# A seven-product matrix step in a decoder layer: one sum of weight blocks by an accumulating DMA, more such steps, and one more block in the ring

## The chip, the cores and the metric

The kernel runs on one core of one Trainium2 chip. Its time is the device time in microseconds of one execution. Before the change three runs gave 1696.13, 1696.37 and 1696.46 us; the median, 1696.37 us, is the number to compare with. The chip profiler recorded one further execution.

The engines are called PE (matrix products; PEld is its weight loading), DVE (element-wise work on tensors), ACT (activation functions and copies), POOL (here a few small operations and the DMAs that its queue issues) and SP (which only issues DMAs). SBUF is the on-chip memory, PSUM the memory that PE writes its sums to.

## The reference

The layer works on 256 tokens of width 2048, all in float32:

```python
h = h + 0.5 * swiglu(rmsnorm(h, ffn1_norm), ffn1_w_in, ffn1_w_out)
u = rmsnorm(h, mix_norm) @ w_in_mix            # pool part, q, k, v, gate, low-rank decay
h = h + concat(pool_mixer(u), gla_mixer(u)) @ w_out_mix
h = h + 0.5 * swiglu(rmsnorm(h, ffn2_norm), ffn2_w_in, ffn2_w_out)
out = rmsnorm(h, final_norm)

def swiglu(h, w_in, w_out):                    # w_in 2048 x 11264, w_out 5632 x 2048
    gate, up = split(h @ w_in)
    return (silu(gate) * up) @ w_out
```

Nearly all work is in the two feed-forward parts: each has 23 million weights in `w_in` and 11.5 million in `w_out`, applied to only 256 rows. The mixer between them has five smaller projections, a pooling branch and a linear attention over chunks of 64 tokens.

## The kernel before

**Precision.** PE multiplies float32 numbers with one rounded factor at a time, so every operand x is kept as two tiles: `hi`, x rounded to PE's format, and `lo`, the rest x - hi. A product of blocks is three matmuls, hi*hi + hi*lo + lo*hi (the function `three`, L193). The activations' pairs stay in SBUF. Weights are read once: a step's weights arrive in a raw slot (`ring_raw`, loaded by SP at L137), ACT casts them to `ring_hi` (L157), DVE subtracts for `ring_lo` (L158).

**Steps.** The tokens are two tiles of 128 rows, the output columns of a group two tiles of 512, and the inner dimension is taken 256 at a time. A step is therefore a 2 x 2 block matrix of activations times a 2 x 2 block matrix of weights (4 blocks of 128 x 512, 1 MB). There are two ways to do it:

- an S step (`Group.s`) does the eight block products, 24 matmuls, and needs the four weight blocks as they are: 4 ring blocks;
- a W step (`Group.w`) does seven products by Winograd's variant of Strassen's scheme, 21 matmuls, with sums of blocks on both sides. The sums of activations (S1 to S4, tiles `s_f`, `s_z`) are made once for each 256-deep slice and used in every chunk. The sums of weight blocks (T1 to T4) are made by DVE for every step, in place in the raw slot, at L181 (`less` in `w_step`). It takes 7 ring blocks: B11, B22, B21 and T1 to T4. Four products go to separate PSUM banks (`pw_...`), and at the end of a group DVE combines them (`combine`, L307 to L310) and adds them to the accumulators (L495).

**Stages.** Each feed-forward part (function `ffn`; names with `f` for the first, `z` for the second) goes through 11 chunks of 512 hidden columns. `first_product(c)` multiplies by `w_in`, eight steps whose kinds stand in `KINDS`, then SiLU, the product with the up half, transposes on PE (`ftp`, `ztp`) and a split into hi and lo. After each chunk but the first and the last, `second_product` multiplies two finished chunks by one half of `w_out` in four S steps (two after chunk 1), halves the result on ACT (`half_f`, `half_z`) and adds it to `hd` in DRAM by an accumulating DMA that POOL issues (L549). The period of the middle of either part is thus one chunk and four S steps. The last two second products keep their result on the chip. `finish2` applies the last norm.

**Buffers.** In the feed-forward parts there are 4 raw slots (3 in the mixer and in the very last group) and a ring of 22 blocks (16 in the mixer and in the last groups), used in turn (class `Ring`); a step whose blocks straddle the ring's end is split into smaller instructions. The order of instructions on each engine is fixed when the program is built, by a scheduler that follows a model of their times; at run time every engine goes through its own list, in order, with semaphore waits. SP's list holds the loads, POOL's the `hd` additions.

The lines that the change touches most:

## Time and profile before

| | |
|---|---|
| median of three runs | 1696.37 us |
| the profiled execution, its own time | 1695.52 us |
| its span, first to last instruction | 1693.7 us |
| PE busy | 1680.2 us |
| DVE busy | 1485.8 us |
| ACT busy | 1022.3 us |
| POOL busy | 69.2 us |
| mean busy share of the 16 DMA engines in the middle of the second feed-forward part | 0.70 to 0.71 |
| granted PE clock, mean over the span | 0.998 of full speed |

A row of the groups reads: line, engine, operation, output<-inputs, shapes, count, then busy time, mean duration in ns, idle time before and what ended it. A matmul's duration (390 ns) overlaps that of the next; what counts is the distance of two starts. A row of the waits reads: who waited, for whom, us in total, times, the longest. A row of the windows reads: the window and its length, then for PE, PEld, DVE, ACT and POOL the busy time and the number of instructions, then the granted clock, the DMA engines' share and GB/s. A row of the DMA issues gives the count, the size of one and the median time from issue to landing.

### The profile page before, as it was taken

The page shows a single profiled execution, that of the slowest core. Times are in us where ns is not written, and L with a number is a line of the kernel's source. Part 1 is how long each engine was busy: PE and PEld are TensorE (multiplying, and loading weights), DVE is VectorE, ACT ScalarE, POOL GpSimd, SP SyncE. Part 2 cuts the span into 40 slices and gives each one's busy share as a digit, 9 for nine tenths or more (in the row PEclk, how much of TensorE's full clock was granted, in tenths as well). Part 3 has the DMA queues.
Part 4 walks back from the last instruction along what each step waited for, and adds up shares of the span by engine and source line. Part 5 has one row for each costly group of instructions (what it writes and reads, how often), then busy time and mean ns, then how long its engine had stood idle before and what let it go on. Part 6 is the DMA issues. An engine that isn't in the chain of part 4 may idle for free.

```text
span 1693.7 us, 21023 instructions
## 1 busy us (share of the span) xinstructions
PE 1680.2 (99%) x7669; PEld 1396.0 (82%) x7669; DVE 1485.8 (88%) x1663; ACT 1022.3 (60%) x1310; POOL 69.2 (4%) x74
## 2 busy tenths in 40 slices
PE   9999999999999999999999999999999999999997
PEld 7888888888888888888898888888888888888886
DVE  8779999999999996767968888999999999999974
ACT  7656666665665664565566565566566566566643
POOL 0000000000000000000000000000000000000012
PEclk9999999999999999999999999999999999999999
DMA  9856756856867776654576484767767667577681
GB/s 344 346 142 226 244 167 236 260 166 235 258 170 223 262 208 235 230 177 140 193 236 230 148 293 152 217 227 218 212 221 227 204 235 235 176 241 242 204 292 51
DMA packets 106330, 369.50 MB, mean 218 GB/s; under 512 B 11873, under 2 KB 15073, under 8 KB 106226
## 3 DMA queue, kind: packets, MB, share of 16 engines
q1 hardware_dynamic: 97026, 335.63, 57.8%
q0 software_dynamic: 8480, 31.46, 8.8%
q8 instruction: 60, 0.98, 0.2%
q10 hardware_dynamic: 720, 1.07, 0.2%
q14 instruction: 44, 0.36, 0.1%
HBM read 340.85 MB, written 27.26 MB: 217 GB/s over the span
## 4 chain that ended last, share of the span: by engine, by line
PE 97%; DMA 1%; DVE 0%; issue 0%; ACT 0%; SPq 0%; POOL 0%; POOLq 0%; DVEq 0%; ACTq 0%
PE ps_fi L193 18%; PE ps_zi L193 16%; PE ps_fo L193 14%; PE ps_zo L193 14%; PE pw_zi L193 9%; PE pw_fi L193 9%; PE ps_h L193 4%; PE pw L193 2%; PE ps_mg L193 2%; PE ps_mv L193 2%; PE ps_mp L193 2%; PE ps_mq L193 1%; PE ps_w_mk L193 1%; PE ps_w_mgr L193 1%; DMA ring_raw<-in_ffn_w_in 1%; PE ztp L511 1%
## 5 line engine op out<-in xcount | busy, mean ns | idle before, releaser
L157 ACT CAST ring_hi<-ring_raw 128x1024 fp32r<-128x1024 f32 (+3 forms) x952 | 837.7, 921 | 524.5 <-DMA ring_raw<-in_ffn_w_in 75.5
L158 DVE TENSOR_TENSOR ring_lo<-ring_raw,ring_hi 128x1024 fp32r<-128x1024 f32 (+5 forms) x794 | 964.3, 1242 | 154.4 <-ACT ring_hi L157 153.7
L181 DVE TENSOR_TENSOR ring_raw<-ring_raw 128x512 f32<-128x512 f32 (+1 forms) x366 | 313.3, 869 | 0.9
L193 PE MATMUL ps_fi<-ring_lo,xT_hi 128*128 128x512 f32 x386 | 150.5, 390 | 0.0
L193 PE MATMUL ps_fi<-ring_hi,xT_hi 128*128 128x512 f32 x386 | 147.8, 391 | 1.6 <-ACT ring_hi L157 1.6
L193 PE MATMUL ps_fi<-ring_hi,xT_lo 128*128 128x512 f32 x386 | 149.4, 389 | 0.0
L193 PE MATMUL ps_zi<-ring_lo,h_hi 128*128 128x512 f32 x362 | 141.0, 389 | 0.0
L193 PE MATMUL ps_zi<-ring_hi,h_lo 128*128 128x512 f32 x362 | 140.9, 390 | 0.0
L193 PE MATMUL ps_zi<-ring_hi,h_hi 128*128 128x512 f32 x362 | 139.7, 390 | 0.5 <-DVE h_mid L1040 0.5
L193 PE MATMUL ps_fo<-ring_lo,fhi 128*128 128x512 f32 x352 | 138.1, 392 | 0.0
L193 PE MATMUL ps_fo<-ring_hi,flo 128*128 128x512 f32 x352 | 137.3, 391 | 0.0
L193 PE MATMUL ps_fo<-ring_hi,fhi 128*128 128x512 f32 x352 | 137.0, 391 | 0.0
L193 PE MATMUL ps_zo<-ring_hi,zhi 128*128 128x512 f32 x344 | 134.9, 392 | 0.0
L193 PE MATMUL ps_zo<-ring_hi,zlo 128*128 128x512 f32 x344 | 134.8, 392 | 0.0
L193 PE MATMUL ps_zo<-ring_lo,zhi 128*128 128x512 f32 x344 | 134.3, 390 | 0.5 <-DVE ring_lo L158 0.5
L193 PE MATMUL pw_zi<-ring_hi,s_z 128*128 128x512 f32 x342 | 116.2, 389 | 0.0
L193 PE MATMUL pw_fi<-ring_hi,s_f 128*128 128x512 f32 x318 | 108.5, 389 | 0.0
L193 PEld LDWEIGHTS ps_fi<-ring_hi,xT_hi 128*128 128x128 f32 x386 | 72.5, 188 | 17.3 <-ACT ring_hi L157 2.3
L193 PEld LDWEIGHTS ps_fi<-ring_lo,xT_hi 128*128 128x128 f32 x386 | 72.6, 188 | 15.6 <-DVE ring_lo L158 0.7
L193 PEld LDWEIGHTS ps_fi<-ring_hi,xT_lo 128*128 128x128 f32 x386 | 72.6, 188 | 15.0
L193 PEld LDWEIGHTS ps_zi<-ring_hi,h_hi 128*128 128x128 f32 x362 | 68.0, 188 | 14.9 <-ACT ring_hi L157 0.9
L193 PEld LDWEIGHTS ps_zi<-ring_hi,h_lo 128*128 128x128 f32 x362 | 67.9, 188 | 14.0
(331 smaller groups left out, 2572.2 us busy)
## 6 DMA issues: line engine op xcount, KB each, us to landing
ring_raw<-in_ffn_w_in SPq DMA_DIRECT2D x350, 512.0 KB, 5.3
ring_raw<-in_ffn_w_out SPq DMA_DIRECT2D x176, 512.0 KB, 5.6
ring_raw<-in_w_out_mix SPq DMA_DIRECT2D x32, 512.0 KB, 5.0
hd<-half_f POOLq DMA_DIRECT2D x18, 512.0 KB, 8.1
hd<-half_z POOLq DMA_DIRECT2D x18, 512.0 KB, 8.3
ring_raw<-in_w_mv SPq DMA_DIRECT2D x16, 512.0 KB, 4.3
ring_raw<-in_w_mp SPq DMA_DIRECT2D x16, 512.0 KB, 4.7
ring_raw<-in_w_mg SPq DMA_DIRECT2D x16, 352.0 KB, 3.6
```

The costliest lines, as they stand in the source:

```text
L157: nc.scalar.copy(out=hi[:, j:k, :], in_=src[:, i + j : i + k, :])
L158: nc.vector.tensor_tensor(out=lo, in0=src[:, i : i + n, :], in1=hi.bitcast(F32), op=ALU.subtract)
L181: nc.vector.tensor_tensor(out=out, in0=x, in1=y, op=ALU.subtract)
L193: nc.tensor.matmul(ps, x, y, start=start and i == 0, stop=stop and i == 2, **kw)
L511: nc.tensor.transpose(tp[:, t, k, :], a_t[t][:, k * P : (k + 1) * P], ident)
```

## The change

1. **The weight sums of a W step.** The blocks of a step lie in memory in another order (B12, B11, B22, B21 instead of B11, B12, B22, B21; the array is built on the host). When the first half is loaded, POOL issues a DMA that reads B11 once more from DRAM (256 KB) and adds it onto B12 in the raw slot. The four sums are rewritten around that block (called Q1; signs in `combine` turn accordingly), so that DVE does two subtractions, one of 512 and one of 1024 columns, instead of three.
2. **More W steps.** Chunks 3 to 10 of both parts have seven W steps and one S step instead of six and two. Chunk 1 of the first part has three W steps instead of none. The last group of all (`zo`, chunks 9 and 10 by the second half of `w_out`) does its two steps of chunk 9 as W steps. This needs a seventh set of activation sums, made in chunk 2 and written over parts of the activations that are not read any more, and sums of chunk 9's hidden columns.
3. **The ring** has 23 blocks in the feed-forward parts instead of 22; one block is skipped at two places (`SKIP`).
4. **Order in the mixer.** The decay factors are computed inside the projection for v, which now precedes that for q; the attention scores move into the projection for the pooling branch.
5. **Small buffers**: `tmp` has three buffers under one tag instead of two under each of two tags.
6. **The end**: the last scalings of the output are held behind the last addition to h (`issue_after`).

```diff
-W_PAIRS = (1, 3, 4, 6, 2, 5)
-CHUNKS = ("WWWWWWSS",) * 8
+W_PAIRS = (1, 3, 4, 6, 2, 5, 0)
+CHUNKS = ("WWWWWWWS",) * 8
 KINDS = {
-    "f": ("SSSSSSSS", "SSSSSSSS", "WWSWWWSS") + CHUNKS,
+    "f": ("SSSSSSSS", "SSSWSWWS", "WWSWWWSS") + CHUNKS,
     "z": ("SSSSSSSS", "SWSWWWSS", "WWSWWWSS") + CHUNKS,
 }
...
-MORE_RING = 6
+MORE_RING = 7
...
+SKIP = {("f", 1): 1, ("f", 2): 1}
+SEVENTH_AT = 2
+SUMS_AT = 2
+LAST = {"f": (2, 3, 0, 1), "z": (0, 1, 2, 3)}
+LAST_W = (9,)
...
-        return lambda k, n: b[n if k == 0 else 3 - n]
+        return lambda k, n: b[1 - n if k == 0 else 3 - n]
...
         w = load(src).rearrange("p (b c) -> p b c", c=CW)
-        f = dict(zip(("B11", "B22", "B21"), parts_of(w, (slice(0, 1), slice(2, 4)))))
+        nc.gpsimd.dma_start(out=w[:, 0, :], in_=src[:, CW : 2 * CW], accum_op=ALU.add)
+        f = dict(zip(("B11", "B22", "B21"), parts_of(w, (slice(1, 2), slice(2, 4)))))
...
-        less(w[:, 0:2, :], w[:, 1:2, :].broadcast_to([P, 2, CW]), w[:, 0:4:2, :])
-        less(w[:, 2, :], w[:, 2, :], w[:, 0, :])
-        less(w[:, 3, :], w[:, 3, :], w[:, 2, :])
-        f.update(zip(("T1", "T3", "T2", "T4"), parts_of(w, PAIRS)))
+        less(w[:, 2, :], w[:, 0, :], w[:, 2, :])
+        less(w[:, 1:4:2, :], w[:, 1:4:2, :], w[:, 2:3, :].broadcast_to([P, 2, CW]))
+        f.update(zip(("Q1", "T3", "T2", "T4"), parts_of(w, PAIRS)))
...
+            if h and np_ == 1 and not first:
+                steps = [steps[i] for i in LAST[name]]
+                kinds = ["W" if c in LAST_W else "S" for c, pr in steps]
...
+                grp.w(a, o_in[kp], w_step(src), True)
...
-    adds = [block([P, 2, CW], F32, f"mv_add{t}") for t in range(NT)]
-    out_of(wide(hact, io["w_mv"], mix_order, W_MIX, h_in, "mv", adds, {5: scores}), v)
...
+    out_of(wide(hact, io["w_mv"], mix_order, W_MIX, h_in, "mv", adds, {5: decay}), v)
+    keys()
...
+        with tc.issue_after(last_add[0]):
...
-        b = np.stack([b[:, :, :, 0, 0], b[:, :, :, 0, 1], b[:, :, :, 1, 1], b[:, :, :, 1, 0]], 3)
+        b = np.stack([b[:, :, :, 0, 1], b[:, :, :, 0, 0], b[:, :, :, 1, 1], b[:, :, :, 1, 0]], 3)
```

How the instructions stand on the engines, at three places. First DVE in the first feed-forward part, around one W step of a late chunk; `ring_raw_134` is the fourth raw slot and holds the step in question, `ring_raw_73` the other three. Before (the step's last two `ring_lo` rows follow further down):

```order
L158 TENSOR_TENSOR ring_lo_75<-ring_raw_134,ring_hi_74 128x512
L158 TENSOR_TENSOR ring_lo_75<-ring_raw_134,ring_hi_74 128x1024
L181 TENSOR_TENSOR ring_raw_73<-ring_raw_73 128x512
L158 TENSOR_TENSOR ring_lo_75<-ring_raw_73,ring_hi_74 128x1024
L181 TENSOR_TENSOR ring_raw_134<-ring_raw_134 128x1024
L181 TENSOR_TENSOR ring_raw_73<-ring_raw_73 128x512
L158 TENSOR_TENSOR ring_lo_136<-ring_raw_73,ring_hi_135 128x512
L181 TENSOR_TENSOR ring_raw_134<-ring_raw_134 128x512
L517 TENSOR_TENSOR flo7_3307<-ftp7_3297,fhi7_3306 128x4x128
L158 TENSOR_TENSOR ring_lo_75<-ring_raw_134,ring_hi_74 128x1024
L181 TENSOR_TENSOR ring_raw_73<-ring_raw_73 128x1024
L181 TENSOR_TENSOR ring_raw_134<-ring_raw_134 128x512
```

With the change:

```order
L167 TENSOR_TENSOR ring_lo_75<-ring_raw_134,ring_hi_74 128x512
L167 TENSOR_TENSOR ring_lo_136<-ring_raw_134,ring_hi_135 128x1024
L191 TENSOR_TENSOR ring_raw_134<-ring_raw_134 128x512
L167 TENSOR_TENSOR ring_lo_136<-ring_raw_73,ring_hi_135 128x512
L191 TENSOR_TENSOR ring_raw_134<-ring_raw_134 128x2x512
L546 TENSOR_TENSOR flo8_3759<-ftp8_3749,fhi8_3758 128x4x128
L167 TENSOR_TENSOR ring_lo_75<-ring_raw_73,ring_hi_74 128x1024
L167 TENSOR_TENSOR ring_lo_136<-ring_raw_134,ring_hi_135 128x1024
L191 TENSOR_TENSOR ring_raw_73<-ring_raw_73 128x512
L167 TENSOR_TENSOR ring_lo_136<-ring_raw_134,ring_hi_135 128x1024
```

The three subtractions have become two, and the first of them (`128x512`) comes right behind the splits of B11, B22 and B21; it is the instruction that waits for the accumulating DMA, with the next step's instructions behind it.

Second POOL in the second feed-forward part. Before, its list holds only the additions to `hd`:

```order
L549 DMA hd<-half_z_8373 128x1024
L549 DMA hd<-half_z_8376 128x1024
L549 DMA hd<-half_z_8800 128x1024
L549 DMA hd<-half_z_8803 128x1024
L549 DMA hd<-half_z_9227 128x1024
```

With the change the block sums (L187) stand among them:

```order
L599 DMA hd<-half_z_8793 128x1024
L187 DMA ring_raw<-in_ffn_w_in 128x512
L599 DMA hd<-half_z_8796 128x1024
L187 DMA ring_raw<-in_ffn_w_in 128x512 x6
L599 DMA hd<-half_z_9220 128x1024
L187 DMA ring_raw<-in_ffn_w_in 128x512
```

Of a chunk's seven sums one stands between the two additions of a second product and two behind the second; the other four stand ahead of the first.

Third DVE at the end of the program (`zh_...` is h, `fin_v` and `fin_r` the last norm's factors, `pre` a partial sum). Before:

```order
L1127 SCALAR_TENSOR_TENSOR zh_11671<-zh_11671,fin_r_12010,gf_11683 128x512
L1127 SCALAR_TENSOR_TENSOR zh_11671<-zh_11671,fin_r_12010,gf_11680 128x512
L1092 TENSOR_REDUCE pre_12014<-ss_h_7225 128x1
L1071 SCALAR_TENSOR_TENSOR zh_11671<-ps_zo_9_last,zh_11671 128x512
L1095 TENSOR_SCALAR pre_12014<-pre_12014 128x1
L1101 SCALAR_TENSOR_TENSOR fin_v_12015<-ss_h_7225,pre_12014 128x1
```

With the change:

```order
L1121 SCALAR_TENSOR_TENSOR zh_11663<-ps_zo_9_last,zh_11663 128x512
L1178 SCALAR_TENSOR_TENSOR zh_11663<-zh_11663,fin_r_12041,gf_11675 128x512
L1178 SCALAR_TENSOR_TENSOR zh_11663<-zh_11663,fin_r_12041,gf_11672 128x512
L1151 SCALAR_TENSOR_TENSOR fin_v_12046<-ss_h_7216,pre_12045 128x1
L1156 SCALAR_TENSOR_TENSOR fin_v_12046<-fin_v_12046,fin_r_12057 128x1
```

The first row tile's two output scalings have moved from ahead of the last addition to h to behind it, ahead of the second tile's `fin_v`.

More of the change, by code (lines that the diff above doesn't have):

```diff
@@ L407, in s_factors, with make @@
         tiles = []
-        def make(kp):
+        def make(kp, spots=None):
             i = kps.index(kp)
-            while len(tiles) <= i // 2:
+            while spots is None and len(tiles) <= i // 2:
                 n = len(tiles)
@@ L530, in second_product @@
             )
-            for c, pr in steps:
+            for i, (c, pr) in enumerate(steps):
                 hi, lo = hidden[c]
@@ L539, in second_product @@
                 src = w_out[np_, kp]
-                grp.s(a, s_step(src))
+                if h and np_ == 0 and not first and i == SUMS_AT:
+                    kps = [x for y in LAST_W for x in (2 * y, 2 * y + 1)]
+                    make = s_factors(
+                        lambda kp: tuple(x[:, 2 * (kp % 2) : 2 * (kp % 2) + 2, :] for x in hidden[kp // 2]),
+                        kps, f"{name}o", (("f", "s2"),),
+                    )
+                    o_in.update((x, make(x)) for x in kps)
+                if kinds[i] == "S":
+                    grp.s(a, s_step(src))
+                    continue
+                grp.w(a, o_in[kp], w_step(src), True)
+                if grp.left_w == 0:
+                    for t in range(NT):
+                        to = h[np_][:, t, :]
+                        nc.vector.scalar_tensor_tensor(
+                            out=to, in0=grp.add[t].rearrange("p n c -> p (n c)"), scalar=0.5, in1=to,
+                            op0=ALU.mult, op1=ALU.add,
+                        )
             if h:
@@ L831, in layer @@
         )
-    h_make = s_factors(pair_of(*hT1), W_MIX, "mix", (("h", "h0"), ("h", "h1")))
-    h_in = {kp: h_make(kp) for kp in W_MIX}
-    mix_order = [kp for kp in range(KD // 2) if kp not in W_MIX]
-    mix_order = mix_order[:2] + list(W_MIX) + mix_order[2:]
     sT = block([P, NT, HEADS, P], F32, "sT")
@@ L1064, in layer @@
     ss3 = small.tile([P, NT, 4], F32, tag="ss", name="ss_h3")
+    last_add = [None]
     def finish2(np_, grp, h):
```

181 lines of the change are left out of this document (106 added, 75 removed).

## The prediction

> **What bounds the kernel now.** I read the busy shares first, then the chain of waits, PE's own waits, and the period of the late chunks.
>
> ```profile
> PE 1680.2 (99%) x7669; PEld 1396.0 (82%) x7669; DVE 1485.8 (88%) x1663; ACT 1022.3 (60%) x1310; POOL 69.2 (4%) x74
> PE 97%; DMA 1%; DVE 0%; issue 0%; ACT 0%; SPq 0%; POOL 0%; POOLq 0%; DVEq 0%; ACTq 0%
> PE ps_fi L193 <- ACT ring_hi L157: 1.6, 1, 1.6
> PE idle L587 <- DVE zeros L582: 1.2, 1, 1.2
> PE ps_zi L193 <- DVE h_mid L1040: 0.5, 1, 0.5
> PE ps_zo L193 <- DVE ring_lo L158: 0.5, 1, 0.5
> 911.48 41.96 PE ps_h L193 x185
> ```
>
> The four waits are all that PE has: 3.8 us. The chain is PE for 97% of the span. A busy PE need not be PE at its peak, so I check the pace: in the last row (the chain, in order of time) 185 matmuls take 41.96 us, 0.2268 us each. The late chunks show the same pace, by the window of one period (a chunk and four S steps) in the second feed-forward part:
>
> ```profile
> 1311.12:1373.29 62.17, 62.17 (x279) 51.48 (x279) 59.21 (x62) 38.38 (x45) 1.72 (x2) 1.00 0.71 223
> ```
>
> Six W and two S steps and four more S steps are 6 x 21 + 6 x 24 = 270 matmuls, 61.24 us at 0.2268, and eight transposes fill the rest of 62.17. So PE never waits in the period, and **fewer matmuls shorten it one for one, as long as the others keep up**. DVE is close behind: 59.21 of 62.17 us. The DMA engines are at 0.71, the clock at 1.00.
>
> **What it removes.** A W step has three matmuls fewer than an S step. Steps turned from S to W: 3 in chunk 1 and 8 in the late chunks of the first part, 8 in the second part, 2 in the last group: 21. 21 x 3 = 63 matmuls x 0.2268 = **14.3 us**. The period becomes 62.17 - 0.68 = 61.49 us.
>
> **What DVE has to do.** Its operations, by form:
>
> ```profile
> L158 DVE TENSOR_TENSOR ring_lo<-ring_raw,ring_hi 128x1024 fp32r<-128x1024 f32 x373 | 451.2, 1224 | 48.3 <-ACT ring_hi L157 48.0
> L158 DVE TENSOR_TENSOR ring_lo<-ring_raw,ring_hi 128x2048 fp32r<-128x2048 f32 x127 | 290.4, 2293 | 69.2 <-ACT ring_hi L157 69.1
> L181 DVE TENSOR_TENSOR ring_raw<-ring_raw 128x512 f32<-128x512 f32 x244 | 167.4, 691 | 0.5
> L158 DVE TENSOR_TENSOR ring_lo<-ring_raw,ring_hi 128x512 fp32r<-128x512 f32 x235 | 160.9, 691 | 14.9 <-ACT ring_hi L157 14.5
> L181 DVE TENSOR_TENSOR ring_raw<-ring_raw 128x1024 f32<-128x1024 f32 x122 | 149.4, 1225 | 0.3
> ```
>
> A W step costs DVE 0.691 + 3 x 1.224 for the splits and, before, 1.225 + 2 x 0.691 for the subtractions: 6.97 us; with the change one subtraction of 0.691 is gone: 6.28. An S step costs 2.29. A period's steps were 6 x 6.97 + 6 x 2.29 = 55.6 and become 7 x 6.28 + 5 x 2.29 = 55.4. (These sums lie above what the window holds, since successive durations overlap by some 0.09 us; the difference of the two is what counts.) So **DVE's work per period stays at 59.2 us, now of 61.49: 2.3 us to spare** where there were 3.0. Inside the stretch of W steps it is eased: it fell behind PE's 21 x 0.2268 = 4.76 us by 2.21 us a step, six times (13.3), now by 1.52, seven times (10.6). The seventh sums and those of chunk 9, some 3 us of DVE each, come three or four times in all, beside S steps; nothing on the path, and 3 us each if that cover were gone. ACT gets three more blocks a period, under 2 us on an engine at 38.4 of 62.17.
>
> **The new DMA.** No row shows an accumulation into SBUF. The nearest ones:
>
> ```profile
> ring_raw<-in_ffn_w_in SPq DMA_DIRECT2D x350, 512.0 KB, 5.3
> hd<-half_f POOLq DMA_DIRECT2D x18, 512.0 KB, 8.1
> hd<-half_z POOLq DMA_DIRECT2D x18, 512.0 KB, 8.3
> ring_raw<-in_w_mp SPq DMA_DIRECT2D x16, 512.0 KB, 4.7
> out<-zh SPq DMA_DIRECT2D x4, 256.0 KB, 2.9
> 1214.05 0.85 POOL L549 DMA_DIRECT2D hd<-half_z  x1 [58.60 <-ACT half_z L546]
> 1214.77 0.71 DVE L181 TENSOR_TENSOR ring_raw<-ring_raw 128x512 f32<-128x512 f32 x1
> 1216.77 0.85 POOL L549 DMA_DIRECT2D hd<-half_z  x1 [1.87 <-ACT half_z L546]
> ```
>
> Between 2.9 us (256 KB, plain) and 8.3 us (512 KB, accumulating into DRAM) from issue to landing; I take 8.3, since that is the same operation, and add POOL's 0.85. By the Trainium skill ("DMA: Bandwidth & Descriptors", section on the anatomy of one DMA: about 2.0 us plus the bytes at 436 GB/s) it would be an estimate of 2.6 us; no run here shows it.
>
> Does the wait reach PE? In its list DVE comes to the waiting subtraction right behind the splits of B11, B22 and B21, and what is queued behind it is the next step's split, for which PE waits. What decides is whether the slot was loaded early enough:
>
> ```profile
> SPq L137 <- DVE ring_lo L158: 312.4, 111, 9.0
> ACT ring_hi L157 <- PE pw_zi L193: 27.8, 18, 2.4
> ACT ring_hi L157 <- PE ps_zo L193: 18.6, 22, 1.2
> DVE ring_lo L158 <- ACT ring_hi L157: 17.0, 24, 1.9
> ```
>
> These are waits over six late periods (373 us). SP waits 312 us for DVE to release a slot, so a slot is reloaded the moment it is free; and ACT waits for PE to free ring blocks, so the splitters are often ahead by the whole ring. From release to a finished sum pass 5.3 + 0.85 + 8.3 = 14.5 us; meanwhile DVE works through the other three slots, 3 x 6.28 = 18.8 us. **The sum lands some 4 us before DVE asks for it**; I take no wait. In the mixer there are three slots: 4.7 + 0.85 + 8.3 = 13.9 against 2 x 6.28 = 12.6, 1.3 us late per W step, 5 us over four in a row, while 16 blocks of ring are 2.3 W steps or 10.9 us of PE's work: hidden too. POOL's sums behind `hd` additions are the fifth to seventh of a chunk, while PE is at the first: about 4 x 4.76 = 19 us of room for 9.
>
> **The DMA engines.**
>
> ```profile
> q1 hardware_dynamic: 97026, 335.63, 57.8%
> q0 software_dynamic: 8480, 31.46, 8.8%
> ```
>
> 57.8% of 1693.7 us for 335.63 MB is 2.92 us per MB; 8.8% for 31.46 MB is 4.74. Seven sums (1.835 MB) at 4.74 add 8.7 us to 0.71 x 62.17 = 44.1: 52.8 of 61.49, 86%. If the 36 additions to `hd` (18.9 MB) carry all of q0's excess, they cost 5.9 us per MB, and it is 90%. Not a bound by either price.
>
> **Start, mixer, end.** In chunk 1 the three W steps need the PSUM banks of chunk 0, and PE's list has chunk 0's transposes 17 matmuls later than before (3.9 us); no wait follows from that. The mixer's moves remove no work: 0, and up to 0.5 us back from PE's waits. At the end the chain changes:
>
> ```profile
> 1683.59 0.39 PE L193 MATMUL ps_zo_last<-ring_hi,zlo 128*128 128x512 f32 x1
> 1682.34 2.45 DVE L1127 SCALAR_TENSOR_TENSOR zh<-zh,fin_r,gf 128x512 f32<-128x512 f32 x2
> 1684.78 0.68 DVE L1071 SCALAR_TENSOR_TENSOR zh<-ps_zo_last,zh 128x512 f32<-128x512 f32 x1
> 1686.24 0.16 DVE L1101 SCALAR_TENSOR_TENSOR fin_v<-ss_h,pre 128x1 f32<-128x1 f32 x1 [0.73 <-ACT sq_h L359]
> ```
>
> The last addition to h waited for the two scalings, 0.8 us past PE's end at 1683.98. Now it starts at 1684.0, the scalings behind it end at 1684.0 + 0.6 + 2.45 = 1687.1, and `fin_v` comes there instead of at 1686.24: **0.9 us more**.
>
> **Sum**, against the profiled execution's own 1695.52 us (1.8 us of it outside the span): 1695.52 - 14.3 + 0.9 = 1682.1. That execution lies 0.85 us under the median of 1696.37, so the forecast is **1683.0 us**.
>
> **Rivals.**
>
> *The gain leaks at the edges* (chunk 1 with three W steps held at once, twelve W steps of the mixer on three slots, the last group behind the final gains on POOL). For: the ring is not full at these places, so the mixer's lateness need not be hidden: 3 groups x 1.3 to 5 us, less overlap, 4 to 10 us: 1687 to 1693. Against: PE has under 4 us of waits there today.
>
> *DVE stands before every sum*, and the kernel is slower. Place: the subtraction behind the splits, in the late chunks. DVE's spare time is 2.3 us a period; a wait of 0.33 us per W step eats it, and from 0.42 us (2.3 + 0.68 = 2.98, over 7) a period is longer than before. At 0.5 us: 3.5 - 2.3 = 1.2 us on 16 periods, 19 us: 1702. For it: 4 us of room on a guessed 8.3 us, an engine that runs its list in order, and slots at the turn from S to W steps that come later than in the stretch. Against: ACT's waits for PE, which say that splitters have room to catch up.
> A rule of the Trainium skill speaks for it ("SBUF - State Buffer", the two separate sides, box on DVE and DMAs from GpSimd): while DVE holds the port pair that it shares with POOL, POOL can't write descriptors. By that rule each issue would wait for the DVE operation in progress, an estimate of 1.2 us. The trace does not agree so far: POOL's issue takes 0.85 us beside DVE's 0.71.
>
> *The DMA engines become the bound.* Break-even is (61.49 - 44.1) / 1.835 = 9.5 us per MB. If a sum costs twice the upper price, since it reads its target too, 11.8 us per MB, a period takes 65.8: 16 x 4.3 = 69 us, 1752. Only partly so (a price near break-even: queues almost full, loads late in the stretch of W steps), half a microsecond to one is lost per period, 8 to 16 us: 1691 to 1699, about no change. Against: additions to `hd` also read their target.
>
> That the change doesn't do what it says is excluded by the lists: PE's has 63 matmuls fewer.
>
> **How the numbers follow.** Forecast 0.62 (1681 to 1687), edges 0.18 (1687 to 1693), DVE before the sums 0.10, DMA engines 0.10 (0.08 of it near no change). About 0.2% (3.4 us) can be told from no change: faster is under 1693.0, up to 1699.8 is the same. Faster 0.62 + 0.18 = 0.80; slower 0.10 + 0.02 = 0.12; same 0.08. The range runs from 1680.5 (the sum, with PE's three short waits at work gone, 2.6 us) to 1693, where the edges end; both slower cases lie outside it.
>
> **What would show it.** Right: PE waits still under 5 us, the period 61.5, DVE about 59 in it, and no DVE wait on a DMA at the first subtraction. The edges: PE waits around chunk 1, in the mixer or in the last 80 us. DVE: waits of `ring_raw` on `ring_raw<-in_ffn_w_in` above 2.3 us a period, and PE waiting for `ring_lo`. The DMA engines: a share near 1.0 and loads far above 5.3 us. A landing above 8.3 + 4 us, or a period at or above 62.17, would make the forecast wrong.

## The result, and the profile after

The changed kernel takes **1722.11 us** (median of four runs, 1716.89 to 1724.48) against 1696.41 us before (four runs, 1696.13 to 1697.50). The ratio is 1.0141, with a 95% interval of 1.0127 to 1.0155: slower by 1.4%. The forecast was 1683.0 us, so 39.1 us are to be explained: 13.4 that were not gained and 25.7 that were lost. The profiled execution is the fastest of the four, 1716.89 us.

The page of the changed kernel (busy time, chain of waits by engine, DMA queues, DMA issues):

```profile
PE 1676.7 (98%) x7606; PEld 1384.1 (81%) x7606; DVE 1506.4 (88%) x1633; ACT 1048.0 (61%) x1319; POOL 195.9 (11%) x217
...
q1 hardware_dynamic: 97026, 335.63, 57.4%
q0 software_dynamic: 29072, 68.96, 21.2%
...
PE 57%; DVE 16%; DMA 15%; issue 7%; ACT 3%; SPq 0%; POOL 0%; DVEq 0%; ACTq 0%; POOLq 0%
...
ring_raw<-in_ffn_w_in SPq DMA_DIRECT2D x350, 512.0 KB, 6.3
...
ring_raw<-in_ffn_w_in POOLq DMA_DIRECT2D x129, 256.0 KB, 6.7
```

PE has 63 instructions fewer, but its work fell by 3.5 us of busy time and the span grew by 20.9. The chain, 97% PE before, now runs through DVE, loads and ACT for a third of the span. The sums land after 6.7 us; the plain loads of `w_in` need 6.3 us instead of 5.3.

What PE waits for in the changed kernel:

```profile
PE ps_fo L202 <- DVE add_fi L327: 9.7, 8, 3.8
PE ps_zo L202 <- DVE add_zi L327: 5.9, 8, 1.7
PE ftp L540 <- DVE fa L528: 3.2, 2, 1.7
PE ps_h L202 <- DVE h_mid L1089: 2.2, 1, 2.2
```

All of PE's waits are 27.4 us now, where they were 3.8. Sixteen of them, as many as there are seven-W chunks, are for L327, the first addition of `combine`. Two late periods (the columns are those of the prediction's window):

```profile
282.51:345.19 62.68, 61.78 (x275) 50.85 (x275) 59.26 (x59) 39.96 (x47) 7.69 (x9) 1.00 0.87 247
1461.63:1524.06 62.43, 61.78 (x275) 50.80 (x275) 59.27 (x59) 39.77 (x47) 7.82 (x9) 1.00 0.89 248
```

DVE's 59.3 us and the DMA engines' 0.87 to 0.89 are what the prediction said; the period is not 61.49.

The starts of the second products on PE's timeline divide the loss. "Forecast" is the length before less 0.2268 us for each matmul that is gone.

| stretch | before | forecast | after | over forecast |
|---|---|---|---|---|
| start to the second product behind chunk 2 | 148.3 | 146.3 | 151.0 | 4.7 |
| first period with a seven-W chunk, first part | 62.2 | 61.5 | 67.5 | 6.0 |
| the next seven periods | 435.0 | 430.2 | 439.8 | 9.6 |
| end of the first part, mixer, chunks 0 and 1 of the second | 432.9 | 432.9 | 435.7 | 2.8 |
| to the second product behind chunk 2 | 51.9 | 51.9 | 53.6 | 1.7 |
| first seven-W period, second part | 62.2 | 61.5 | 64.4 | 2.9 |
| the next seven periods | 435.2 | 430.4 | 438.1 | 7.7 |
| to the last matmul | 55.9 | 54.5 | 53.9 | -0.6 |

They add up to 34.8 us, which is 1716.89 against the 1682.1 forecast for a profiled execution.

How such a wait comes about is best seen where it is longest. The timelines of ACT, DVE and PE of the changed kernel in the first seven-W chunk (start, duration, and in brackets the idle time before and what ended it):

```profile
209.97 1.05 ACT L166 CAST ring_hi<-ring_raw 128x1024 fp32r<-128x1024 f32 x1 [4.21 <-DMA ring_raw<-in_ffn_w_out]
211.69 3.46 ACT L166 CAST ring_hi<-ring_raw 128x1024 fp32r<-128x1024 f32 x4 [0.67 <-DMA ring_raw<-in_ffn_w_out]
215.06 0.57 ACT L326 COPY add_fi<-pw_fi 128x512 f32<-128x512 f32 x1
```

```profile
212.77 5.10 DVE L167 TENSOR_TENSOR ring_lo<-ring_raw,ring_hi 128x2048 fp32r<-128x2048 f32 x3 [2.84 <-ACT ring_hi L166]
217.78 0.68 DVE L327 TENSOR_TENSOR add_fi<-pw_fi,add_fi 128x512 f32<-128x512 f32 x1
```

```profile
214.32 0.39 PE L202 MATMUL ps_fi<-ring_hi,xT_lo 128*128 128x512 f32 x1
218.52 0.80 PE L202 MATMUL ps_fo<-ring_hi,fhi 128*128 128x512 f32 x1 [3.81 <-DVE add_fi L327]
219.11 0.63 PE L202 MATMUL ps_fo<-ring_lo,fhi 128*128 128x512 f32 x1
219.54 0.63 PE L202 MATMUL ps_fo<-ring_hi,flo 128*128 128x512 f32 x1
```

The second product's accumulators `ps_fo` take the PSUM banks of the four single products `pw_fi`. These are free when ACT has copied one and DVE has added the next. In both lists these instructions stand behind the casts and splits of the S steps that follow. Here a load of `w_out` lands late (ACT waited 4.21 us for it), DVE starts its splits at 212.8, and the addition comes at 217.8. PE's list holds 14 matmuls between the last `pw` matmul and the first of the second product, 3.2 us; before, with two S steps at a chunk's end instead of one, it held 26 in the second part, 5.9 us, and 27 to 44 in the first. These matmuls are called the cover of the combine below.

### The profile page after: what moved, and what is told of

It reads as the page before. It is cut to its first block, busy times and chain, and to the rows that moved or that the text cites. A ratio compares the mean times of both kernels' runs of the same rounds, so it can differ in the third digit from the quotient of the medians.

```text
span 1714.6 us, 21473 instructions
## 1 busy us (share of the span) xinstructions
PE 1676.7 (98%) x7606; PEld 1384.1 (81%) x7606; DVE 1506.4 (88%) x1633; ACT 1048.0 (61%) x1319; POOL 195.9 (11%) x217
## 3 DMA queue, kind: packets, MB, share of 16 engines
q0 software_dynamic: 29072, 68.96, 21.2%
## 4 chain that ended last, share of the span: by engine, by line
PE 57%; DVE 16%; DMA 15%; issue 7%; ACT 3%; SPq 0%; POOL 0%; DVEq 0%; ACTq 0%; POOLq 0%
PE ps_zo L202 13%; PE ps_fo L202 12%; DVE ring_lo L167 11%; DMA ring_raw<-in_ffn_w_in 7%; PE ps_fi L202 7%; DMA ring_raw<-in_ffn_w_out 7%; PE ps_zi L202 6%; DVE ring_raw L191 4%; PE pw_zi L202 3%; PE pw_fi L202 3%; ACT ring_hi L166 3%; PE ps_mp L202 2%; DMA ring_raw<-in_w_out_mix 2%; PE ps_mv L202 2%; PE pw L202 2%
## 5 line engine op out<-in xcount | busy, mean ns | idle before, releaser
L166 ACT CAST ring_hi<-ring_raw 128x1024 fp32r<-128x1024 f32 (+2 forms) x949 | 859.2, 949 | 476.4 <-DMA ring_raw<-in_ffn_w_out 86.6
L167 DVE TENSOR_TENSOR ring_lo<-ring_raw,ring_hi 128x1024 fp32r<-128x1024 f32 (+5 forms) x802 | 993.1, 1271 | 141.3 <-ACT ring_hi L166 137.0
L191 DVE TENSOR_TENSOR ring_raw<-ring_raw 128x512 f32<-128x512 f32 (+1 forms) x286 | 272.1, 953 | 15.0 <-DMA ring_raw<-in_ffn_w_in 13.0
L187 POOL DMA_DIRECT2D ring_raw<-in_ffn_w_in x129 | 111.1, 861 | 937.7 <-DMA ring_raw<-in_ffn_w_in 557.0
L202 PE MATMUL ps_fi<-ring_hi,xT_hi 128*128 128x512 f32 x328 | 125.3, 391 | 1.6 <-ACT ring_hi L166 1.6
L202 PE MATMUL ps_fi<-ring_hi,xT_lo 128*128 128x512 f32 x328 | 126.7, 390 | 0.0
L202 PEld LDWEIGHTS ps_fo<-ring_hi,fhi 128*128 128x128 f32 x352 | 66.5, 189 | 26.4 <-DVE add_fi L327 13.0
L202 PEld LDWEIGHTS ps_zo<-ring_hi,zhi 128*128 128x128 f32 x338 | 63.5, 188 | 24.5 <-DVE add_zi L327 9.3
L202 PEld LDWEIGHTS ps_fo<-ring_hi,flo 128*128 128x128 f32 x352 | 66.4, 189 | 13.7
L202 PEld LDWEIGHTS ps_fo<-ring_lo,fhi 128*128 128x128 f32 x352 | 66.6, 189 | 13.1
```

The costliest lines, as they stand in the source:

```text
L166: nc.scalar.copy(out=hi[:, j:k, :], in_=src[:, i + j : i + k, :])
L167: nc.vector.tensor_tensor(out=lo, in0=src[:, i : i + n, :], in1=hi.bitcast(F32), op=ALU.subtract)
L187: nc.gpsimd.dma_start(out=w[:, 0, :], in_=src[:, CW : 2 * CW], accum_op=ALU.add)
L191: nc.vector.tensor_tensor(out=out, in0=x, in1=y, op=ALU.subtract)
L202: nc.tensor.matmul(ps, x, y, start=start and i == 0, stop=stop and i == 2, **kw)
```

## The experiments

Times are medians; the kernel before ran beside each set (1697.40 to 1698.31 us), and ratios are to it. The scheduler orders the lists of each kernel anew, so an edit also moves other instructions. The expectations give letters to the theories: A, the wait for these banks; B, the DMAs of the sums; C, chunk 1; E, splitters that are late as a whole, so that the wait only changes its place; F, the combine's place in the lists.

### What the accumulating DMA costs

Edits: `no_sum` is the changed kernel without the DMA; `sum_6w` is the kernel before with the DMA and the two subtractions that go with it (six W steps, ring of 22).

```diff
-        nc.gpsimd.dma_start(out=w[:, 0, :], in_=src[:, CW : 2 * CW], accum_op=ALU.add)
```

```diff
...
         w = load(src).rearrange("p (b c) -> p b c", c=CW)
+        nc.gpsimd.dma_start(out=w[:, 0, :], in_=src[:, CW : 2 * CW], accum_op=ALU.add)
...
-        less(w[:, 0:2, :], w[:, 1:2, :].broadcast_to([P, 2, CW]), w[:, 0:4:2, :])
-        less(w[:, 2, :], w[:, 2, :], w[:, 0, :])
-        less(w[:, 3, :], w[:, 3, :], w[:, 2, :])
+        less(w[:, 2, :], w[:, 0, :], w[:, 2, :])
+        less(w[:, 1:4:2, :], w[:, 1:4:2, :], w[:, 2:3, :].broadcast_to([P, 2, CW]))
```

> The changed kernel without the accumulating DMA: the line that adds B11 onto B12 in the raw slot is left out, so Q1 is B12 alone (that part of the computation is missing); W steps, ring, orders in the program text as in the changed kernel. Theory A (the time goes where PE waits for the PSUM banks that held the four single products: one S step less between the last of them and the second product, whatever the DMA does): the period in late chunks stays at 62.3 to 62.9 us, the waits of PE for the combine (first addition of the single products) stay at 0.4 to 1.3 us a period, total 1710 to 1722. Theory B (the accumulating DMA makes slots and loads late, and the combine stands behind late splits): the waits go below 0.2 us, the period is 61.5, loads are back at 5.3 us, and the total is 1681 to 1690.

> The kernel before with the accumulating DMA alone (block order, two subtractions instead of three, signs in the combine); six W steps, ring of 22, everything else as before. Theory A: the cover of the combine is as before (26 matmuls), PE has under 6 us of waits, the period is 62.17, total 1695 to 1698. Theory B: the late slots show here too: waits of PE for the combine or for ring blocks of 0.5 us and more in every period, total 1702 to 1715.

`no_sum` 1713.23 us, 1.0086 [1.0056, 1.0115]; `sum_6w` 1719.56 us, 1.0118 [1.0094, 1.0141]. `sum_6w` lies above the ranges of both theories, so neither stands alone. Without any sum the waits for the combine are still there (`no_sum`, PE's waits):

```profile
PE ps_fo L201 <- DVE add_fi L326: 12.6, 8, 4.4
PE ps_zo L201 <- DVE add_zi L326: 6.1, 7, 1.8
```

And the DMA alone, with DVE eased by a subtraction and at least 26 matmuls of cover, makes the kernel before slower by 1.2%. One of its late periods, by the window and by ACT's waits in it:

```profile
337.10:401.70 64.60, 63.01 (x279) 51.28 (x279) 56.76 (x57) 38.11 (x50) 7.02 (x9) 1.00 0.82 237
```

```profile
ACT ring_hi L157 <- DVE ring_raw L182: 10.6, 4, 2.9
ACT ring_hi L157 <- DMA ring_raw<-in_ffn_w_in: 8.0, 1, 8.0
ACT ring_hi L157 <- DMA ring_raw<-in_ffn_w_out: 6.6, 4, 2.3
```

DVE has 56.8 of 64.6 us to do, and ACT waits for loads and subtractions but no longer for PE: the ring's lead is gone, though no engine's share is near 1.

Is it the chain (load, then sum, then subtraction) or the traffic? `sum_eighth` is `sum_6w` with 64 of the 512 columns in each DMA, `eighth_7w` the same in the changed kernel; `turn_dve` lets DVE add in the first two W steps of a chunk of `sum_6w`.

```diff
...
+        nc.gpsimd.dma_start(out=w[:, 0, 0:64], in_=src[:, CW : CW + 64], accum_op=ALU.add)
...
```

> The kernel before with the accumulating DMA alone (the run sum_6w, 1719.6), but only 64 of the 512 columns of B11 are added; the rest of the sum is left out. POOL's issue, the wait for the load before it and DVE's wait behind it stay; seven eighths of the traffic go. If the serial chain at the turn (load, then sum, then DVE) costs the time: 1712 to 1720, with periods of the first feed-forward part of 63.5 us or more. If the traffic does (longer loads, 0.83 of the DMA engines): loads back at 5.3 to 5.8 us, periods of 62.2, total 1697 to 1703.

> The changed kernel with the accumulating DMA on 64 of the 512 columns (the rest of the sum is left out). If the traffic of the sums costs here as in the six-W kernel, this is like the run with no sum at all, 1710 to 1716, against 1722. If the waits for the sums cost (issue, landing, DVE behind it), it stays at 1718 to 1724.

> The kernel before with the accumulating DMA alone (the run sum_6w, 1719.6), but the first two W steps of each group make their sum on DVE instead (0.69 us more of DVE each, as many operations as before the change). Theory B at the turn (all four slots come free together when S steps end; the loads and then the sums behind them land together 12 to 14 us later, and DVE stands): without sums at the turn the loss goes: total 1696 to 1703. If the loss comes from the sums in the stretch, or from the DMA traffic as such (6 x 0.26 MB a period less a third): 1710 to 1718.

`sum_eighth` 1701.11 us, 1.0020 [1.0011, 1.0029]; `eighth_7w` 1710.70 us, 1.0066 [1.0049, 1.0084]; `turn_dve` 1705.92 us, 1.0049 [1.0034, 1.0064]. The small DMA has the same issue, semaphores and place in the lists, and the period of the six-W kernel is back (`sum_eighth`):

```profile
335.10:397.20 62.10, 62.10 (x280) 51.50 (x278) 56.09 (x57) 38.00 (x48) 7.00 (x8) 1.00 0.75 223
```

So **the bytes cost; issue, semaphores and order do not**. The bytes act in two ways that these runs do not part: plain loads of `w_in` need 6.3 us in `sum_6w` and 5.4 in `sum_eighth`, and the sum itself lands after 5.8 us in the one and 4.0 in the other, where DVE's 12.2 us of waits for sums are gone. By the ratios the traffic costs 0.0098 +- 0.0025 of 1697 us, 16.6 us, in the six-W kernel and 0.0075 +- 0.0022, 12.7 us, in the changed one. The traces place only a part of the latter: mixer, entry of the second part and its late periods of `eighth_7w` lose 6.7 us less than the changed kernel's, but its first part's seven late periods lose more (its profiled execution, 1714.96 us, is the slowest of its four). `turn_dve`, with four of a chunk's six sums by DMA, loses 8.5 us where `sum_6w` loses 22.1. That lies between its two expected ranges: the first two sums of a chunk, behind the S steps, cost more than their third of the bytes.

Why a mean share of 0.87 was no assurance shows the DMA view of one period, 40 slices of 1.6 us; first the kernel before, then the changed one:

```profile
DMA  9999300450378204999999781835379998997799
```

```profile
DMA  9999999277999877799999369930299899999999
```

Seventeen slices were at 0.9 or more before, 27 are after. Loads are asked for when slots come free, in bursts; that a load is delayed by the burst that it falls into, and not by the mean, is the reading that fits.

### The seven-W chunk

In `s_behind` the S step's matmuls stand behind the last `pw` product, so that 26 matmuls cover the combine; `no_sum_behind` is the same without the DMA.

```diff
...
-                    grp.s(a_of(kp), b)
+                    if c > 2 and grp.with_w and grp.left_w == 0:
+                        with tc.issue_after(grp.last_pw):
+                            grp.s(a_of(kp), b)
+                    else:
+                        grp.s(a_of(kp), b)
```

> The changed kernel with the one S step of chunks 3 to 10 held in PE's list behind the last of the single products: 26 matmuls between that and the second product instead of 14, as before the change. Theory A: 12 matmuls more of cover are 2.7 us, more than the waits of 0.5 to 1.3 us; they vanish, period 61.5 to 61.8, total 1700 to 1708. Theory E: PE now waits for the last W step's sums instead (pw waits for ring_lo or ring_hi of 0.5 to 1.3 us in each period), total 1715 to 1722.

> The changed kernel without the accumulating DMA (B11 is not added, that part of the computation is left out) and with the S step of late chunks behind the last single product in PE's list (26 matmuls of cover for the combine). It joins the two runs that took one away each (1713 and 1722). Theory A+B (cover and sums each hide the other): with both away PE has no wait left in the late chunks, 61.5 us a period, total 1685 to 1692. Theory E (seven W steps in a row run DVE's lead out, whatever else): the wait for the combine turns into waits for ring_lo of 0.5 to 1 us, period 62.2 to 62.8, total 1705 to 1716.

`s_behind` 1722.55 us, 1.0140 [1.0123, 1.0157]; `no_sum_behind` 1715.08 us, 1.0097 [1.0081, 1.0112]: nothing gained by more cover. In `s_behind` the waits for `add_fi` fall from 9.7 to 6.0 us, but those of `pw` products for `ring_lo` come to 8.5. PE's waits in `no_sum_behind` show the same:

```profile
PE ps_fo L201 <- DVE add_fi L327: 7.5, 4, 2.8
PE pw_zi L201 <- DVE ring_lo L167: 4.5, 6, 0.8
PE pw_fi L201 <- DVE ring_lo L167: 3.6, 8, 1.8
```

PE now waits for splits in the W stretch. So the bank is where the delay shows, not its only cause. Next, is DVE too slow? `lean` has no DMA and leaves out DVE's second subtraction as well:

```diff
-        nc.gpsimd.dma_start(out=w[:, 0, :], in_=src[:, CW : 2 * CW], accum_op=ALU.add)
...
-        less(w[:, 1:4:2, :], w[:, 1:4:2, :], w[:, 2:3, :].broadcast_to([P, 2, CW]))
```

> The changed kernel without the accumulating DMA and without DVE's second subtraction (1.22 us a W step, 8.6 us a period): B11 is not added and T2, T4 and B-sums that hang on it are not formed, that part of the computation is left out. Theory E (DVE late at the end of a stretch of seven W steps is what costs 16 us in the run without sums): waits of PE for the combine and for ring_lo go, period 61.5 us, total 1682 to 1690. If something else is late there (ACT's copies, the slots, PE's order): 62.2 us or more a period, total 1702 to 1714.

1707.88 us, 1.0053 [1.0035, 1.0071]: the rival's range. Two of its periods, and ACT's timeline ahead of the end of the first:

```profile
460.40:523.26 62.86, 61.71 (x275) 50.86 (x275) 51.70 (x52) 39.79 (x46) 1.74 (x2) 1.00 0.70 218
1267.20:1328.80 61.60, 61.60 (x277) 51.04 (x277) 51.68 (x52) 39.71 (x47) 1.72 (x2) 1.00 0.72 224
```

```profile
516.43 3.47 ACT L166 CAST ring_hi<-ring_raw 128x1024 fp32r<-128x1024 f32 x4 [4.79 <-DMA ring_raw<-in_ffn_w_out]
519.80 0.58 ACT L324 COPY add_fi<-pw_fi 128x512 f32<-128x512 f32 x1
```

With DVE at 51.7 of 62 us and no sums on the DMA engines, some periods run at the forecast pace and others wait for the combine as before, behind a load of `w_out` that lands 4.8 us after ACT asks. And that with more cover, since the scheduler put 27 matmuls there in this kernel. **DVE's rate is at most a small part of the cause**: `lean` is 5.4 us faster than `no_sum`, which the two intervals do not tell from 0.

Why that load is late can be read from the chain that ends at this wait (the chain in order of time: start, duration, what):

```profile
503.75 0.69 PE pw_fi L200 x3
504.47 1.06 ACT ring_hi L166
...
507.76 1.23 DVE ring_lo L167
...
509.01 7.32 DMA ring_raw<-in_ffn_w_out
...
516.43 1.06 ACT ring_hi L166
...
521.93 0.68 DVE ring_lo L167
522.61 0.61 DVE add_fi L325
...
523.26 2.79 PE ps_fo L200 x11
```

PE frees a ring block at 504.44, ACT and DVE fill it, DVE's split frees a raw slot, the load into that slot takes 7.3 us, and its casts and splits stand ahead of the addition for which PE waits. The way round takes 18.8 us, and PE had 17.7 us of work in its list. In the changed kernel it goes through two loads in several periods: from 446.70 to 470.25 and from 1438.52 to 1461.63, 23.5 and 23.1 us. By these chains, what ran out is time on a round trip through the ring and the raw slots, and no engine is fully busy on it. It agrees with this that an S step holds PE for 6 matmuls per ring block and a W step for 3, so that a ring full of W steps is the shorter lead. No run with a longer ring and the same slots tests it.

Four more edits tried to cure it. In `act_copy` ACT evacuates both pairs of banks and DVE combines from SBUF; in `raw5` there are five raw slots and a ring of 21; in `comb3` the cast and split of the second product's fourth step and of the next chunk's first are issued behind the combine's copy and first addition; `comb3_c1s` also has chunk 1 of the first part back in S steps.

```diff
...
+                for x, to in zip(self.pair, (c, d)):
+                    nc.scalar.copy(out=to, in_=x)
...
```

```diff
-MORE_RAW = 1
-MORE_RING = 7
+MORE_RAW = 2
+MORE_RING = 5
```

```diff
...
+                    if not h and len(chunks) == 2 and chunks[-1] > 1 and i == 3:
+                        with tc.issue_after(freed[0]), tc.issue_after(freed[1]):
+                            b = s_step(src)
...
```

> The changed kernel with one change in the combine: ACT copies both tiles of the four single products (1024 columns each) to SBUF at once, so the PSUM banks are free after ACT, without DVE; DVE combines from SBUF. Cover in PE's list stays at 14 matmuls. Theory A (every seven-W period loses 0.5 to 4 us because DVE's combine, late behind splits, holds the banks): PE's waits for the combine go (25 us in the changed kernel's trace: 9.7 + 5.9 + 1.6 waited at the combine's lines and what the late start of the accumulators draws after it), period 61.5 to 61.8 us, total 1700 to 1708. Theory E (DVE itself is late; if PE does not wait for the combine it waits for the next splits a few matmuls later): the waits move to ring_lo or ring_hi, period 62.2 to 62.8, total 1715 to 1722.

> The changed kernel with five raw slots and a ring of 21 blocks in the feed-forward parts (instead of four and 23, the same room). Theory B (slots are held 6 us longer by the accumulating DMA, so loads come late and with them the splits and the combine): loads are issued a step earlier, ACT's waits for loads fall by half or more, waits of PE under 0.4 us a period, total 1698 to 1708. Theory A: loads come earlier but the combine stays behind splits and the ring is two blocks shorter: total 1714 to 1724.

> The changed kernel with the splits of the fourth second-product step and of the next chunk's first step queued behind the combine's copy (ACT) and first addition (DVE), which so stand 2560 columns, some 2.9 us of DVE, earlier in the lists. Theory F (the combine's place in the lists, behind splits whose loads come late, holds the banks): PE's waits for the combine, 0.5 to 1.3 us a period, go, the period is 61.6 to 61.9 us, total 1704 to 1712. Rival (in-order engines only swap who stands: ACT and DVE now stand for PE's last single product, and the splits behind them are late a few microseconds after): period 62.2 or more, total 1716 to 1725.

> The run f_c1_s (chunk 1 of the first feed-forward part in S steps, 1720.1) with the combine moved up as in comb3. Theory F: periods of 61.6 to 61.9 us, total 1700 to 1710, still above the kernel before by the traffic of the sums (9 to 11 us between the run with an eighth of them and the changed kernel) less what seven W steps save. Rival: 1715 to 1722.

`act_copy` 1771.24 us, 1.0432 [1.0404, 1.0460]; `raw5` 1719.06 us, 1.0131 [1.0116, 1.0146]; `comb3` 1752.84 us, 1.0331 [1.0314, 1.0348]; `comb3_c1s` 1743.62 us, 1.0269 [1.0242, 1.0295]. None of the four is a cure; `raw5` lies where it was expected if the combine stays behind the splits, the other three above every range. In `act_copy` PE's longest waits became those for ACT's casts (14.9 us for `pw_fi`). In `comb3` the waits for the combine stay (12.2 us for `ps_fo`), and ACT waits 148.4 us for loads of `w_in` where the changed kernel has 46.9. The reading that fits is that the splits held back release the raw slots later, and so the next loads are late.

`raw5` has a flaw of its own: 69 blocks of a period do not divide by 21, so steps straddle the ring's end and DVE has 51 instructions more. Yet it has a period without a single wait of PE beside a slow one:

```profile
1339.83:1401.40 61.57, 61.57 (x275) 50.82 (x275) 59.21 (x62) 39.26 (x49) 7.85 (x9) 1.00 0.84 248
1275.65:1339.83 64.18, 62.48 (x276) 50.53 (x276) 58.83 (x59) 39.95 (x47) 7.84 (x9) 1.00 0.84 243
```

So 61.5 us can be run with this work on every engine, but not every time. A fifth slot with a ring that divides 69 was not tried.

### Who else could add the blocks

`dve_sum` and `pool_sum` are the changed kernel with the sum made by DVE and by POOL (the edit for POOL; for DVE the new line begins `nc.vector`):

```diff
-        nc.gpsimd.dma_start(out=w[:, 0, :], in_=src[:, CW : 2 * CW], accum_op=ALU.add)
...
+        nc.gpsimd.tensor_tensor(out=w[:, 0, :], in0=w[:, 0, :], in1=w[:, 1, :], op=ALU.add)
```

> The changed kernel with B11 added onto B12 by DVE (one addition of 512 columns per W step) in place of the DMA. DVE's work per period becomes 59.3 + 7 x 0.69 = 64.1 us, more than PE's 61.5, so DVE is the bound: period 64 to 65, total 1740 to 1765 if nothing else gives. Theory A and theory B both expect that; they differ in the loads: 5.3 us by B, 6.3 by A if the longer loads come from the second feed-forward part's own pace and not from the sums.

> The changed kernel with the sum B12 + B11 made by POOL as an operation on the raw slot (128 x 512), not by a DMA: no traffic, no wait for a second landing, 1.3 to 2.0 us of POOL a step by the nearest rows (ktail 1.29 us, zh 2.03 us). If only the sum's way matters (theory B), it is like the run without any sum: 1708 to 1716. If POOL's operation and DVE's get in each other's way, DVE's operations in late chunks get longer than 0.69, 1.22 and 2.29 us and the total is above 1722.

`dve_sum` 1825.96 us, 1.0759 [1.0731, 1.0787], well above what was expected of it; `pool_sum` 1787.40 us, 1.0525 [1.0500, 1.0551]. With the sum DVE has 59.3 + 7 x 0.69 = 64.1 us to do in a period of 61.5; in `dve_sum` the periods become 66 to 74 us. By POOL an addition is slow, and so is what DVE does beside it; groups of `pool_sum`, then of the changed kernel:

```profile
L193 POOL TENSOR_TENSOR ring_raw<-ring_raw 128x512 f32<-128x512 f32 x143 | 406.4, 2844 | 796.1 <-DMA ring_raw<-in_ffn_w_in 606.7 <-DVE ring_lo L167 94.9 <-DMA ring_raw<-in_w_out_mix 49.3
...
L190 DVE TENSOR_TENSOR ring_raw<-ring_raw 128x512 f32<-128x512 f32 x143 | 125.1, 875 | 16.8 <-POOL ring_raw L193 14.3
```

```profile
L191 DVE TENSOR_TENSOR ring_raw<-ring_raw 128x512 f32<-128x512 f32 x143 | 98.1, 687 | 14.7 <-DMA ring_raw<-in_ffn_w_in 13.0 <-DMA ring_raw<-in_w_out_mix 0.8
```

The accumulating DMA is the cheapest of the three ways to have the seventh W step.

### The edges

`f_c1_s` is the changed kernel with chunk 1 of the first part in S steps. The other three are the changed kernel with six-W chunks and no accumulating DMA for sums, so that mixer order, last group and chunk 1 are what is left of the change: `edges_only` with a ring of 23 and the block sum added by DVE, `edges22` with the ring of 22, the W step of before and 13 ring blocks skipped once ahead of chunk 1, `last_only` the same with chunk 1 in S steps and no block skipped.

```diff
-    "f": ("SSSSSSSS", "SSSWSWWS", "WWSWWWSS") + CHUNKS,
+    "f": ("SSSSSSSS", "SSSSSSSS", "WWSWWWSS") + CHUNKS,
```

```diff
-CHUNKS = ("WWWWWWWS",) * 8
+CHUNKS = ("WWWWWWSS",) * 8
...
-MORE_RING = 7
+MORE_RING = 6
```

> The changed kernel with chunk 1 of the first feed-forward part in S steps again (and no skipped ring blocks). Theory C (over a third of the loss arises at the start: three W steps in chunk 1 bring the waits of the transposes for fa at 107 and 164 us and a late first seven-W chunk): 9 matmuls more (+2.0 us), but the 10 us lost before 219 us are mostly got back: total 1709 to 1714 against 1717 to 1724. If the start's loss comes from the accumulating DMA or from chunk 3 alone, it stays within 2 us of the changed kernel, 1718 to 1724.

> All of the change but its two main parts: late chunks have six W steps as before, and the sum with B11 is made by DVE (three operations per W step, as before). What is left: three W steps in chunk 1 of the first feed-forward part, two in the last group (15 matmuls fewer, 3.4 us), the ring of 23, the mixer's order, the end. If the edges do what the prediction said (no new wait, 0.9 us lost at the end): 1693 to 1695. If they leak (waits around chunk 1, in the mixer, in the last 80 us, as the first rival has it): 1697 to 1703.

> What is left of the change without its two main parts, this time with the ring of 22 blocks, the operations of a W step as before, and 13 skipped blocks so that late chunks stand on the ring as before: three W steps in chunk 1 of the first feed-forward part, two in the last group, the mixer's order, the buffers, the end. Edges as predicted: 15 matmuls are 3.4 us, 0.9 lost at the end: 1693 to 1695. Edges that leak: 1697 to 1705. If it is near 1745 again, the ring was not the reason of that.

> As edges22, but chunk 1 of the first feed-forward part in S steps (no skipped blocks). 6 matmuls fewer are 1.4 us, 0.9 lost at the end: 1695.5 to 1697 if the mixer's order and the last group cost nothing; 1698 to 1702 if they do. The difference to edges22 is chunk 1's: 2.0 us in favour of edges22 by the prediction, some 2 to 6 us against it if the waits of the transposes for fa come with the three W steps.

`f_c1_s` 1720.12 us, 1.0136 [1.0121, 1.0151]: the first late second product starts at 210.8 instead of 218.5, but the later periods of the profiled executions lose it again (that of `f_c1_s`, 1723.01 us, is the slowest of its four, the changed kernel's the fastest); chunk 1's cost in the changed kernel is not told from 0. `edges_only`, 1745.30 us, 1.0273 [1.0259, 1.0287], tells nothing on the edges: 66 blocks of its period do not divide by 23, and steps straddle (DVE has 1710 instructions). `edges22` 1708.17 us, 1.0058 [1.0044, 1.0071]; `last_only` 1698.89 us, 1.0002 [0.9994, 1.0011]. `edges22` is slower than even a leak was expected to make it. So mixer order, last group and end cost nothing that can be measured, and **the three W steps of chunk 1, with the 13 skipped blocks, cost 9.3 us** where the forecast had a gain of 2.0. Some 3.4 us of it are lost by 213 us; the rest comes at the end of the first part, where PE waits 1.0 and 1.9 us at 643 and 646 and ACT waits 12.0 us for loads of `w_out` (5.2 in `last_only`). There the loads issued from 631 to 637 take 9.3 to 10.6 us, while POOL's second read of `hd` (`fh<-hd`, 1 MB) is under way, from 629.8 to 639.7. Chunk 1 need not be the reason: `f_c1_s` has it in S steps and loses as much there (a period of 66.5 us), and the changed kernel, which has it in W steps, does not (62.5).

## Why the prediction was wrong

Point by point, by its own steps.

- **What bounds the kernel**: right for before. "One for one, as long as the others keep up" was the sentence that failed: they did not keep up.
- **63 matmuls, 14.3 us**: the count is right, and `raw5` and `lean` have periods of 61.6 us. The gain is there on PE and is eaten by waits.
- **DVE's work stays at 59.2 us**: right to 0.1. But "2.3 us to spare" was taken as a margin against lateness, and `lean`, with 10 us to spare, waits as well.
- **The new DMA, 14.5 us from release to finished sum, no wait**: a landing of 6.7 instead of 8.3 us, and DVE's waits at the first subtraction are 13.0 us in the whole run. Half right: the time to the finished sum was not underestimated (6.3 + 0.86 + 6.7 = 13.9 us), but the 13 waits are there, and their absence was the prediction's own sign of being right. `sum_eighth` shows that the issue and the order alone are harmless.
- **The DMA engines, 86 to 90%, "not a bound by either price"**: the share came out (0.87 to 0.89), the conclusion did not. The test was a break-even of means, 9.5 us per MB; the queue's extra bytes cost 5.7 (q0 rose from 31.46 to 68.96 MB and from 8.8 to 21.2% of the span), well below it, and still a cost. Loads went from 5.3 to 6.3 us, and the traffic cost 16.6 us in the six-W kernel. This is the mechanism that rival 3 named "only partly so", with 8 to 16 us and a chance of 0.08.
- **Chunk 1, "no wait follows from that"**: wrong. PE waits 1.67 and 1.56 us for DVE's `fa` at 107 and 164 us in the changed kernel, and `edges22` against `last_only` gives +9.3 for the forecast's -2.0, of which only the 3.4 us up to 213 us lie near chunk 1.
- **The mixer hidden, the order in it 0**: 2.8 us over forecast up to chunk 1 of the second part. Whether that is the sums stays open: without any sum it is 0.4 in `no_sum` (659.0 to 1092.3) and 4.3 in `last_only` (645.1 to 1082.3), in `sum_eighth` 5.3 (645.6 to 1083.8). In `last_only` and `sum_eighth` PE waits 3.3 and 3.1 us for `h_mid`.
- **The end, +0.9**: the number came out partly by luck. PE's last matmul starts 20.4 us later, the time is 21.4 us longer; but `fin_v` comes only 0.5 us later behind PE's end, and the other 0.5 lies outside the span. The last addition waits 0.6 us behind PE's end for another DVE operation, and the two scalings take 1.40 us and not 2.45.
- **The rivals**: none named the wait that is most frequent after the change. The prediction turned an S step into a W step and counted its matmuls, its blocks and DVE's work, but not that the S step at a chunk's end was cover for the combine: 26 matmuls and more became 14. That was overlooked, but it is not the cause by itself, since `s_behind` puts 26 back and gains nothing. The rule on POOL's descriptors, which the prediction carried over to DVE's subtractions, was not seen: POOL's issue took 0.86 us on 129 sums.

**The step that failed** is "fewer matmuls shorten it one for one, as long as the others keep up", because keeping up was judged by mean busy time: 2.3 us to spare on DVE, 86 to 90% on the DMA engines. Those means came out, and the late periods took 62.2 to 64.0 us instead of 61.49. What the runs showed in its place are two costs that a mean does not hold: the bytes of the sums, put at nothing, cost 10 to 13 us, and the seven-W chunks lose time without any sum (`no_sum`, 15.4 us in thirteen late periods), where PE waits at the end of a round trip through ring and slots (18.8 us in `lean`).

The account of the 39.1 us, each by its difference to the kernel before beside it: about 10 to 13 the traffic of the sums (`no_sum` recovers 9.9, `eighth_7w` 12.7 by ratios); 1 the mixer order, last group and end (`last_only` +0.6 for -0.5); 5 or so chunk 1 (3.0 + 2.0 by the medians of `f_c1_s`, though its interval does not tell the 3.0 from 0; 3.4 + 2.0 by `edges22` up to 213 us). The rest, 20 to 23 us, is put down to the seven-W chunks themselves by subtraction. `no_sum`, which has no traffic of sums, bears the size out by its windows over the late periods:

```profile
281.73:659.00 377.27, 370.79 (x1651) 305.00 (x1651) 355.76 (x348) 239.47 (x276) 11.88 (x14) 1.00 0.71 222
1207.70:1645.20 437.50, 433.07 (x1926) 355.57 (x1926) 414.40 (x406) 278.74 (x321) 13.53 (x16) 1.00 0.72 222
```

Six periods take 377.27 us and seven 437.50 where 61.49 each would be 368.9 and 430.4: 15.4 us, and the period ahead of the six (65.8 us) adds 4.3. The parts are not strictly additive, since each delay uses up lead that hides another.

What stays open is how to shorten the round trip. Shown is that the loss is there without sums, with more cover, and with a leaner DVE, that moving the combine makes it worse, and which way the chain runs ahead of a wait. That seven blocks a step from a ring of 23 leave too little lead fits the chain; no run varied the ring alone, so it is argued and not shown.

No version here beats the kernel before; `last_only` equals it.

## What to carry to other kernels

When a step is replaced by a shorter one, look up what the longer one covered: count the matmuls between the last use of a PSUM bank and its next, and follow the chain from the buffer that PE frees, through loads and splits, back to PE; its length, and not the busy time on it, must fit into PE's remaining work. A mean share of 0.87 on DMA engines that serve bursts is not room for more; read the slices, and try the new transfer at an eighth of its size to part its bytes from its issue and order (its landing gets shorter too). A ring should divide the blocks of a period before its size is varied, and a cure by reordering in-order queues should be expected to move a wait rather than remove it.

## What was not expected of the hardware

**A stall slows the matmuls that follow it.** After the 3.81 us wait at 218.5 six matmuls start 0.43 us apart instead of 0.2268 (timeline above), and the window has the granted clock at 0.52:

```profile
218.50:221.50 3.00, 2.98 (x7) 2.40 (x8) 3.00 (x4) 0.00 (x0) 0.00 (x0) 0.52 0.98 361
```

It also happened after a shorter idle: 1.67 us, four transposes, 0.54 us, and then matmuls 0.43 us apart from 108.6 to 112.0 us (PE's timeline of the changed kernel):

```profile
107.36 0.66 PE L540 MATMUL ftp<-ident,fa 128*128 128x128 f32 x4 [1.67 <-DVE fa L528]
108.56 0.64 PE L202 MATMUL pw_fi<-ring_hi,xT_hi 128*128 128x512 f32 x1 [0.54 <-ACT half_f L596]
109.00 0.63 PE L202 MATMUL pw_fi<-ring_lo,xT_hi 128*128 128x512 f32 x1
```

Six to eight matmuls at 0.2 us more make 1.2 to 1.6 us on top of such a wait. The wait of 1.56 us at 164 was followed by the full pace. By the Trainium skill ("TensorE: Matmul & The Clock Gate", Part 1) half rate follows a free-running window of about 3.4 us without work, and by its section "Why this matters for your kernels" PE should have no gap above some 3 us. The half rate and its length agree with the traces here (2.7 and 3.4 us of slow starts), but gaps of 1.67 and 0.54 us were enough once.

**POOL and DVE slow each other.** An addition of 128 x 512 floats takes POOL 2.84 us beside DVE, where its product of that size in the mixer (`ktail`), with DVE idle, took 1.29; and DVE's operation of that size 0.875 instead of 0.687 us. The Trainium skill ("SBUF — State Buffer", "Who interferes with whom") says that a DVE instruction with two inputs in SBUF contends with a GpSimd instruction that reads SBUF; the rows agree with that. An accumulating DMA from POOL's queue did not slow DVE: 687 ns against 691 before.
